# Differential attention: scores from two 64-row halves, keys and queries of a head kept on chip

## The chip, the cores and the metric

The kernel runs on one core of one Trainium2 chip. The metric is device time in microseconds (us) of one execution; the median of 3 runs is given, and one further execution is profiled.

## The reference, cut to what matters

The program is a two-layer backbone of a diffusion model: layer 0 mixes tokens by differential attention, layer 1 by a state-space scan, each followed by an MLP. Only the attention core of layer 0 is changed. There are 8 heads, 1024 latent tokens and 256 context tokens. Each head has two components `c` with 64 rows (`ATTN_HD`), whose softmaxes are subtracted:

```python
def attend(q, k, v):
    s = jnp.einsum('bqhcd,bkhcd->bhcqk', q, k).astype(jnp.float32)
    p = jax.nn.softmax(s, axis=-1)
    w = p[:, :, 0] - lam * p[:, :, 1]
    o = jnp.einsum('bhqk,bkhe->bqhe', w.astype(v.dtype), v)
    return rmsnorm(o, subln_g) * (1.0 - lambda_init)
```

Everything is in float32. The kernel gets this from TensorE by splitting each operand into a rounded high part and the remainder (`hi`, `lo`, type fp32r): a product of two operands is hi·hi + hi·lo + lo·hi, three matmuls (`mm3`, lines 131 to 134).

## The kernel before

The changed part is `phase_b`. It runs over 72 units in program order, 9 for each head: unit u=0 takes the 256 context queries against the 256 context keys, units u=1 to 8 take 128 latent queries each against all 1280 keys. The loop is inside `manual()`, so on TensorE, VectorE, ScalarE and GpSimd the instructions stand in the order in which the code writes them.

One unit, in the order of the code:

- `scores` (lines 575 and 581): both components. K of a component is a tile of 128 rows, the 64 hi rows above the 64 lo rows; Q comes in two forms, `r=0` (hi above lo) and `r=1` (lo above hi). Two 128-row matmuls for each piece of at most 512 keys then sum four products, lo·lo among them. A unit with u>0 has 12 matmuls, 8 of 512 columns and 4 of 256, component 0 first.
- `maxima` (590, 594): VectorE copies the scores of a component from PSUM and takes the row extreme; `exps` (601, 604): ScalarE's exponential of each component; `combine` (612 to 615): VectorE subtracts.
- In the *next* unit the combined weights are transposed by TensorE (622, 627) in three parts, T0 (four 128x128 transposes), T1 (two) and T2 (four), and taken out of PSUM by `w_evac`: T0 by ScalarE (hi, 635) and VectorE (lo, 636), T1 and T2 by a ScalarE copy (640) and two GpSimd operations (641, 642).
- `values`: the `mm3` of the transposed weights of two units with V, 30 matmuls of 256 columns (6 after u=0). It stands behind the scores in units u = 1, 4, 6 and 8 (the 6 in u=2). Units u = 3, 5, 7 and 0 have none.
- Projections of the next head's Q and K (`proj_group`, 24 matmuls) fill TensorE between the transposes in u = 0, 1, 2, 3, 5 and 7 (`AHEAD`, `FILLS`); in head 7 the first part of the output projection does.

The place of `w_evac` differs. In most units T0 is taken out right behind its transposes, ahead of the exponentials in ScalarE's queue. In units with 30-matmul `values` ("late" in the code) it stands behind both exponentials and behind `combine`.

PSUM is one tile `PS` of 4096 columns: 8 banks of 512. Component 0 of the scores takes columns 0 to 1279, component 1 columns 1280 to 2559 (banks 0 to 4). T0 and most T2 go to bank 5, `values` and T1 to bank 6, projections (and T2 where there is no projection) to bank 7.

K and Q go through DRAM: `proj_group` splits them into a staging tile `stg` and writes them to `Kd` and `Qd` (`out`), and `load_k` and `load_q` read them back in the stacked forms, K of component 1 of the next head and the first two Q tiles behind the scores of u=8.

Of the kernel before, what the change touches and what calls it, by code (L numbers as in the profile page):

```python
# [10 lines left out]
ALU = mybir.AluOpType  # L11
# [59 lines left out]
class Prog:  # L71
# [430 lines left out]

    def proj_group(self, h, T, g, wt):
# [7 lines left out]
        q, sw, qc, s = self.rq, self.rs, self.rc, self.stg[:, :, 0:n]  # L511

        def product(k):
            return lambda: self.mm3(b, wt[k][0], wt[k][1], hT[0][:, k], hT[1][:, k], k == 0, k == 7)

        def out():
            dst = self.Kd if T else self.Qd
            for c in range(2):
                self.dma(dst[h % 2, c, :, c0 : c0 + n].rearrange("(l r) n -> r l n", l=2),
                         s[64 * c : 64 * c + 64].bitcast(F32))  # L520

        def direct():
            nc.scalar.activation(s[:, 0], b, AF.Copy, scale=scale)
            nc.vector.scalar_tensor_tensor(s[:, 1], b, scale, s[:, 0].bitcast(F32), ALU.mult, ALU.subtract)
            out()

        def evac():
            nc.scalar.activation(q, b, AF.Copy, scale=scale)
            nc.vector.scalar_tensor_tensor(qc, b, scale, self.cosT[:, t], ALU.mult, ALU.mult)
            for j in range(4):  # L530
                self.dma(sw[32 * j : 32 * j + 32], q[32 * (j ^ 1) : 32 * (j ^ 1) + 32])

        def sine():
            nc.gpsimd.tensor_tensor(sw, sw, self.sinT[:, t], ALU.mult)

        def add():
            nc.vector.tensor_tensor(qc, qc, sw, ALU.add)

        def store():
            self.split(s[:, 0], s[:, 1], qc)  # L540
# [25 lines left out]


    def scores(self, u, Q, K):
        mm = self.nc.tensor.matmul
        if u == 0:  # L570
            for t in range(2):
                for c in range(2):
                    o = self.PS[:, 512 * t + 256 * c : 512 * t + 256 * c + 256]
                    for r in range(2):
                        mm(o, Q[:, c, r, 128 * t : 128 * t + 128], K[c][:, 0:256], start=r == 0, stop=r == 1)
            return
        qs = slice(128 * ((u - 1) % 2), 128 * ((u - 1) % 2) + 128)
        for c in range(2):
            for k0, k1 in (((0, 512), (512, 1024), (1024, 1280)), ((0, 256), (256, 768), (768, 1280)))[c]:
                for r in range(2):  # L580
                    mm(self.PS[:, 1280 * c + k0 : 1280 * c + k1], Q[:, c, r, qs], K[c][:, k0:k1], start=r == 0, stop=r == 1)  # L581


    def maxima(self, u, p, sm):
        ts = self.nc.vector.tensor_scalar
        if u == 0:
            for t in range(2):
                for c in range(2):
                    i = 512 * t + 256 * c
                    ts(p[c][:, 256 * t : 256 * t + 256], self.PS[:, i : i + 256], 1.0, None, ALU.mult, ALU.min,  # L590
                       accum_out=sm[:, 2 * t + c : 2 * t + c + 1])
        else:
            for c in range(2):
                ts(p[c], self.PS[:, 1280 * c : 1280 * c + 1280], 1.0, None, ALU.mult, ALU.min, accum_out=sm[:, c : c + 1])  # L594

# [21 lines left out]
    def w_part(self, u, w, n, tb):  # L617

        if u == 0:
            for kt in range(2):  # L620
                for t in range(2):
                    self.nc.tensor.transpose(tb[:, 256 * kt + 128 * t : 256 * kt + 128 * t + 128],
                                             w[:, 256 * t + 128 * kt : 256 * t + 128 * kt + 128], self.ident)
            return shaped(tb, (2, 256)), self.wT[0][:, 0:2], self.wT[1][:, 0:2]
        k0, k1 = ((0, 4), (4, 6), (6, 10))[n]
        for kt in range(k0, k1):
            self.nc.tensor.transpose(tb[:, 128 * (kt - k0) : 128 * (kt - k0) + 128],  # L627
                                     w[:, 128 * kt : 128 * kt + 128], self.ident)
        qs = slice(128 * ((u - 1) % 2), 128 * ((u - 1) % 2) + 128)
        return shaped(tb[:, 0 : 128 * (k1 - k0)], (k1 - k0, 128)), self.wT[0][:, k0:k1, qs], self.wT[1][:, k0:k1, qs]  # L630

    def w_evac(self, tb, hi, lo, direct):
# [4 lines left out]
        else:  # L637
            m, n = tb.shape[1:]
            t = shaped(self.wraw.next()[:, 0 : m * n], (m, n))
            nc.scalar.activation(t, tb, AF.Copy)  # L640
# [11 lines left out]
    def b_start(self):  # L652
# [4 lines left out]
        self.wr = Ring([(self.rv(4 * i, 4, 128), self.rv(4 * i + 2, 4, 128)) for i in range(3)])  # L657
        self.stg = self.rv(12, 2, 512)
        self.qb = Ring([self.bank(i) for i in (4, 5)])
# [4 lines left out]
        for split, T in zip(splits, (1, 0)):  # L664
            split(0)
            wt = split(1)
            for g in (2, 0, 1):
                products, rest = self.proj_group(0, T, g, wt)
                for f in products:
# [9 lines left out]
    def phase_b(self):  # L679
# [6 lines left out]
        self.raw = Ring([self.wv(0, 1024)])  # L686
        Kr = Ring([self.view(self.R1, 5 * i, (1280,)) for i in range(3)])
        Vr = Ring([self.rv(36 + 5 * i, 10, 128) for i in range(3)] + [self.view(self.R1, 15, (10, 128))])
        Qr = Ring([self.rv(51 + 4 * i, 2, 2, 256) for i in range(2)])
        self.wT = self.rv(16, 10, 256), self.rv(26, 10, 256)  # L690
        pb = self.bank(6)
        loaded = {}

        def load_k(h, c):
            K = loaded[h, "k", c] = self.rv(0, 1280) if (h, c) == (7, 1) else Kr.next()
            for k0, k1 in ((0, 256), (256, 1280)):
                self.dma(K[:, k0:k1].bitcast(F32), self.Kd[h % 2, c, :, k0:k1])
# [6 lines left out]
        def load_q(h, pair):  # L704
            Q = Qr.next()
            cols = slice(256 * pair, 256 * pair + 256)
            self.dma(Q[:, :, 0].bitcast(F32), self.Qd[h % 2, :, :, cols].rearrange("c r n -> r c n"))
            for hl in range(2):
                self.dma(Q[64 * hl : 64 * hl + 64, :, 1].bitcast(F32),
                         self.Qd[h % 2, :, 64 - 64 * hl : 128 - 64 * hl, cols].rearrange("c r n -> r c n"))  # L710
            loaded[h, pair] = Q

# [95 lines left out]
        wsums, wt6 = Ring([self.wv(0, 512), self.wv(2, 512)]), []  # L808
        wregs = [(self.view(t, x, (2, 512)), self.view(t, x + 4, (2, 512))) for t, x in ((self.R1, 0), (self.R, 8), (self.R, 36))]
        wraw6 = [shaped(self.wv(x, 1024), (2, 512)) for x in (0, 8, 12)]  # L810
# [41 lines left out]
        self.qb = Ring([self.bank(7)])  # L852
        load_k(0, 0)
        load_k(0, 1)
        load_q(0, 0)
        load_q(0, 1)
        load_v(0)
# [17 lines left out]
        with self.manual():  # L875
            for n in range(72 + 5):
# [10 lines left out]
                if front:  # L887
                    K = loaded[h, 'k', 0], loaded[h, 'k', 1]
                    pair = (u + 1) // 2
                    Q = loaded[h, pair]  # L890
# [1578 lines left out]
    def run(self):  # L2469
        tc = self.tc  # L2470
        pool = lambda name, **kw: tc.tile_pool(name=name, bufs=1, **kw)
        with pool("cst") as self.cst, pool("psp", space=bass.MemoryType.PSUM) as psp, \
             pool("drp", space=bass.MemoryType.DRAM) as drp, pool("hp") as hp:
            dt = lambda name, *shape: drp.tile(list(shape), F32, name=name)
            self.PS = psp.tile([128, 4096], F32, name="PS")
            self.Kd, self.Qd = dt("Kd", 2, 2, 128, 1280), dt("Qd", 2, 2, 128, 1280)
            self.Vd = dt("Vd", 8, 2, 128, 10, 128)
# [17 lines left out]
            with pool("r0") as rp, pool("fc") as cp:  # L2495
# [6 lines left out]
                with pool("r1") as rp, pool("f1") as fp:  # L2502
                    self.R1, self.F1 = rp.tile([128, 20 * KB], F32R, name="R1"), fp.tile([128, int(25.5 * KB)], F32, name="F1")
                    self.phase_b()
# [74 lines left out]
```

## Time and profile before

| | us |
|---|---|
| median of 3 runs (2848.01 to 2848.93) | 2848.92 |
| span of the profiled execution | 2849.8 |
| units of `phase_b`, first scores of head 0 to the end of head 7 | 222.7 to 852.4 |
| of it one head, by 8 | 78.7 |
| matmuls of `scores` in the program (lines 575, 581) | 64 + 768 |

How to read the rows of the profile: times are from the span's start. A row of the timeline has start, duration, engine, line and operation, written tile and read tiles, and a count where neighbours of one line were merged; idle time ahead of an instruction stands in brackets with what ended it. PE is TensorE's matmuls, PEld its weight loads, DVE VectorE, ACT ScalarE, POOL GpSimd. A matmul's duration holds its latency, so in a dense stream the distance from start to start tells the rate. PEclk is the granted share of TensorE's clock.

### The profile page before, as it was taken

The page shows a single profiled execution, that of the slowest core. Times are in us where ns is not written, and L with a number is a line of the kernel's source. Part 1 is how long each engine was busy: PE and PEld are TensorE (multiplying, and loading weights), DVE is VectorE, ACT ScalarE, POOL GpSimd, SP SyncE. Part 2 cuts the span into 40 slices and gives each one's busy share as a digit, 9 for nine tenths or more (in the row PEclk, how much of TensorE's full clock was granted, in tenths as well). Part 3 has the DMA queues.
Part 4 walks back from the last instruction along what each step waited for, and adds up shares of the span by engine and source line. Part 5 has one row for each costly group of instructions (what it writes and reads, how often), then busy time and mean ns, then how long its engine had stood idle before and what let it go on. Part 6 is the DMA issues. An engine that isn't in the chain of part 4 may idle for free.

```text
span 2849.8 us, 43385 instructions
## 1 busy us (share of the span) xinstructions
PE 2723.3 (96%) x15229; PEld 2283.1 (80%) x15229; DVE 2019.8 (71%) x2984; ACT 1369.5 (48%) x2583; POOL 1037.2 (36%) x901
## 2 busy tenths in 40 slices
PE   6999999999999999999999999789999999999999
PEld 4688888888877887778877878688887778888887
DVE  6357788888873667767698878799543597668466
ACT  3425555565653753333444445487444633344443
POOL 3314676766663600000030013688121143336414
PEclk9999999999999999999999999899999999999999
DMA  9955555655825359886799878579742144476544
GB/s 279 319 172 188 152 173 172 177 171 171 256 91 182 128 179 316 294 302 216 249 312 310 272 238 263 169 228 306 235 154 98 66 163 160 155 246 227 167 131 142
DMA packets 414823, 586.30 MB, mean 206 GB/s; under 512 B 41870, under 2 KB 260236, under 8 KB 411404
## 3 DMA queue, kind: packets, MB, share of 16 engines
q1 hardware_dynamic: 414604, 583.52, 63.5%
q8 instruction: 120, 1.97, 0.3%
q14 instruction: 99, 0.81, 0.1%
HBM read 396.38 MB, written 182.82 MB: 203 GB/s over the span
## 4 chain that ended last, share of the span: by engine, by line
PE 76%; DVE 9%; DMA 5%; issue 4%; POOL 3%; ACT 2%; SPq 1%; DVEq 0%; ACTq 0%; POOLq 0%
PE PS L132 21%; PE PS L134 20%; PE PS L133 20%; PE PS L581 4%; PE PS L627 2%; PE PS L1928 2%; PE PS L1963 2%; DMA FU<-in_mlp_w 1%; DMA Ta<-FU 1%; PE PS L202 1%; DVE R L138 1%; SPq L80 1%; DVE F L615 1%; ACT F L604 1%; DVE H L138 1%
## 5 line engine op out<-in xcount | busy, mean ns | idle before, releaser
L132 PE MATMUL PS<-H 128*128 128x512 f32 x1072 | 420.6, 393 | 2.7 <-ACT H L137 1.7
L134 PE MATMUL PS<-H 128*128 128x512 f32 x1072 | 417.5, 390 | 2.8 <-DVE H L138 1.5
L133 PE MATMUL PS<-H 128*128 128x512 f32 x1072 | 417.7, 390 | 0.0
L132 PE MATMUL PS<-H,R 128*128 128x512 f32 (+1 forms) x828 | 308.0, 374 | 4.3 <-ACT R L137 2.0
L133 PE MATMUL PS<-H,R 128*128 128x512 f32 (+1 forms) x828 | 298.6, 361 | 0.0
L134 PE MATMUL PS<-H,R 128*128 128x512 f32 (+1 forms) x828 | 298.0, 361 | 0.0
L132 PEld LDWEIGHTS PS<-H 128*128 128x128 f32 x1072 | 201.2, 188 | 50.5 <-issue 6.4
L134 PEld LDWEIGHTS PS<-H 128*128 128x128 f32 x1072 | 201.2, 188 | 46.1 <-DVE H L138 2.3
L133 PEld LDWEIGHTS PS<-H 128*128 128x128 f32 x1072 | 201.3, 188 | 40.6
L604 ACT ACTIVATE F<-F,stat 128x1280 f32<-128x1280 f32 x128 | 174.3, 1362 | 106.6 <-DVE F L594 106.5
L137 ACT ACTIVATE H<-U 128x640 fp32r<-128x640 f32 x216 | 131.9, 674 | 172.6 <-PE PS L133 138.3
L137 ACT ACTIVATE R<-W 128x512 fp32r<-128x512 f32 (+1 forms) x184 | 128.7, 707 | 174.1 <-PE PS L133 101.5
L132 PE MATMUL PS<-R,H 128*128 128x512 f32 x520 | 208.0, 401 | 3.3 <-ACT H L137 3.3
L134 PE MATMUL PS<-R,H 128*128 128x512 f32 x520 | 205.0, 396 | 1.8 <-DVE H L138 1.8
L133 PE MATMUL PS<-R,H 128*128 128x512 f32 x520 | 204.5, 394 | 0.0
L138 DVE TENSOR_TENSOR H<-U,H 128x640 fp32r<-128x640 f32 x216 | 165.1, 797 | 50.6 <-ACT H L137 49.6
L138 DVE TENSOR_TENSOR H<-W,H 128x512 fp32r<-128x512 f32 (+1 forms) x137 | 125.2, 924 | 102.8 <-ACT H L137 102.1
L594 DVE TENSOR_SCALAR_CACHE_REDUCE F<-PS 128x1280 f32<-128x1280 f32 x128 | 185.2, 1483 | 9.3 <-PE PS L581 9.1
L137 ACT ACTIVATE H<-W 128x512 fp32r<-128x512 f32 (+2 forms) x158 | 95.4, 613 | 188.7 <-PE PS L133 116.8
L132 PEld LDWEIGHTS PS<-H,R 128*128 128x128 f32 x828 | 157.6, 191 | 30.2 <-issue 4.1
L134 PEld LDWEIGHTS PS<-H,R 128*128 128x128 f32 x828 | 157.0, 190 | 25.2 <-issue 0.8
L641 POOL TENSOR_SCALAR R<-F 128x256 fp32r<-128x256 f32 (+1 forms) x128 | 126.5, 989 | 136.0 <-ACT F L640 122.4
(534 smaller groups left out, 6860.0 us busy)
## 6 DMA issues: line engine op xcount, KB each, us to landing
W<-in_mlp_w SPq DMA_DIRECT2D x176, 256.0 KB
U<-Aa SPq DMA_DIRECT2D x108, 320.0 KB
Aa<-FU SPq DMA_DIRECT2D x91, 320.0 KB
Ad<-F SPq DMA_DIRECT2D x112, 256.0 KB
W<-Ad SPq DMA_DIRECT2D x112, 256.0 KB
FU<-in_mlp_w SPq DMA_DIRECT2D x32, 512.0 KB
Ta<-FU SPq DMA_DIRECT2D x16, 1024.0 KB
U<-in_ada_w SPq DMA_DIRECT2D x32, 512.0 KB
```

What stands on the lines that cost most here:

```text
L132: mm(out, ah, bh, start=first, stop=False, **kw)
L133: mm(out, ah, bl, start=False, stop=False, **kw)
L134: mm(out, al, bh, start=False, stop=last, **kw)
L137: self.nc.scalar.activation(hi, src, AF.Copy)
L138: (lo_eng or self.nc.vector).tensor_tensor(lo, src, hi.bitcast(F32), ALU.subtract)
L581: mm(self.PS[:, 1280 * c + k0 : 1280 * c + k1], Q[:, c, r, qs], K[c][:, k0:k1], start=r == 0, stop=r == 1)
L594: ts(p[c], self.PS[:, 1280 * c : 1280 * c + 1280], 1.0, None, ALU.mult, ALU.min, accum_out=sm[:, c : c + 1])
L604: nc.scalar.activation(p[c], p[c], AF.Exp, bias=sm[:, c : c + 1], scale=-1.0, accum_out=sn[:, 0:1] if c else s0[:, u + 1 : u + 2])
L627: self.nc.tensor.transpose(tb[:, 128 * (kt - k0) : 128 * (kt - k0) + 128], w[:, 128 * kt : 128 * kt + 128], self.ident)
L641: nc.gpsimd.tensor_scalar(hi, t, 1.0, 0.0, ALU.mult, ALU.add)
L1928: mm(b[:, o : o + 160], X[:, d, i, 64 * j : 64 * j + 128], U[:, 4 * n + i, cols], start=True, stop=True)
L1963: mm(o, cs[d][n % 2][j][:, i], W[:, d, i], start=False, stop=d == 1 and j == 1)
```

## The change

K and Q of a head no longer go through DRAM (but for head 0): `proj_group` writes hi and lo straight to resident tiles, `Ks[h % 2]` (two heads) and `Qs` (one), in which rows 0 to 63 are component 0 and rows 64 to 127 component 1. The staging tile, `load_k` and `load_q` go, and with them 228 DMAs of the program.

`scores` takes each component from its own 64 rows: hi·hi, hi·lo and lo·hi, three 64-row matmuls for each piece in the place of two 128-row ones, 18 for a unit with u>0 (12 for u=0; 8 before). `score_order` alternates the components, so that neighbouring matmuls mostly use different halves of TensorE's rows and different PSUM banks. For that component 1 moves from column 1280 to column 1536: component 0 has banks 0 to 2, component 1 banks 3 to 5. Bank 5 is no longer free; T0 and T2 now go to `spare`, the last 256 columns of bank 2 and of bank 5. Tiles in SBUF are laid out anew.

```diff
     def proj_group(self, h, T, g, wt, stage=None):
...
+        if stage is None:
+            hi, lo = (x[:, c0 : c0 + n] for x in (self.Ks[h % 2] if T else self.Qs))
+        else:
+            hi, lo = stage[:, 0, 0:n], stage[:, 1, 0:n]
...
         def out():
-            dst = self.Kd if T else self.Qd
-            for c in range(2):
-                self.dma(dst[h % 2, c, :, c0 : c0 + n].rearrange("(l r) n -> r l n", l=2),
-                         s[64 * c : 64 * c + 64].bitcast(F32))
+            if stage is not None:
+                for l, t_ in enumerate((hi, lo)):
+                    self.dma((self.Kd if T else self.Qd)[l, :, c0 : c0 + n], t_.bitcast(F32))
...
+    def score_order(self):
+        items = []
+        for c, chunks in ((0, ((1024, 1280), (0, 512), (512, 1024))), (1, ((0, 512), (512, 1024), (1024, 1280)))):
+            at = c / 8
+            for k in chunks:
+                for j in range(3):
+                    items.append((at, c, k, j))
+                    at += (k[1] - k[0]) / 512
+        return [x[1:] for x in sorted(items)]
...
     def scores(self, u, Q, K):
         mm = self.nc.tensor.matmul
+        half = lambda t, c, k: t[64 * c : 64 * c + 64, k]
+        pairs = ((0, 0), (0, 1), (1, 0))
...
-        qs = slice(128 * ((u - 1) % 2), 128 * ((u - 1) % 2) + 128)
-        for c in range(2):
-            for k0, k1 in (((0, 512), (512, 1024), (1024, 1280)), ((0, 256), (256, 768), (768, 1280)))[c]:
-                for r in range(2):
-                    mm(self.PS[:, 1280 * c + k0 : 1280 * c + k1], Q[:, c, r, qs], K[c][:, k0:k1], start=r == 0, stop=r == 1)
+        qs = slice(128 + 128 * u, 256 + 128 * u)
+        for c, (k0, k1), j in self.order:
+            a, b = pairs[j]
+            mm(self.PS[:, 1536 * c + k0 : 1536 * c + k1], half(Q[a], c, qs), half(K[b], c, slice(k0, k1)), start=j == 0, stop=j == 2)
...
             for c in range(2):
-                ts(p[c], self.PS[:, 1280 * c : 1280 * c + 1280], 1.0, None, ALU.mult, ALU.min, accum_out=sm[:, c : c + 1])
+                ts(p[c], self.PS[:, 1536 * c : 1536 * c + 1280], 1.0, None, ALU.mult, ALU.min, accum_out=sm[:, c : c + 1])
...
         for kt in range(k0, k1):
-            self.nc.tensor.transpose(tb[:, 128 * (kt - k0) : 128 * (kt - k0) + 128],
+            i = kt - k0
+            self.nc.tensor.transpose(tb[:, i // 2, 128 * (i % 2) : 128 * (i % 2) + 128],
...
+        r1 = lambda off, *dims: self.view(self.R1, off, dims)
+        self.Ks = [(r1(10 * i, 1280), r1(10 * i + 5, 1280)) for i in range(2)]
+        self.Qs = self.rv(49, 1280), self.rv(54, 1280)
+        self.order = self.score_order()
+        self.spare = shaped(self.PS[:, 0:3072], (2, 1536))[:, :, 1280:1536]
...
-                        load_k(h + 1, 0)
-                    if u % 2 == 0 and u < 8 and (h, pair + 1) not in loaded:
-                        load_q(h, pair + 1)
...
-                    self.scores(u, Q, K)
-                    if u == 8 and h < 7:
-                        load_k(h + 1, 1)
-                        load_q(h + 1, 0)
-                        load_q(h + 1, 1)
+                    self.scores(u, self.Qs, self.Ks[h % 2])
...
-                        tb = pb[:, 256:512] if part == 1 else self.bank(7 if part == 2 and not groups else 5)
+                        tb = (shaped(pb[:, 256:512], (1, 256)) if part == 1 else
+                              shaped(self.bank(7), (2, 256)) if part == 2 and not groups else self.spare)
```

Three places in the built programs, with the semaphores that each instruction waits for. TensorE in unit 3 of head 3, a unit without `values`, before: the scores (581), T0 (627), the first products of the projection.

```order
L581 MATMUL PS<-R_1850,R_110 128x512 [waits DMAHW7_49]
L581 MATMUL PS<-R_1850,R_110 128x512 [waits DMAHW1_49,DMAHW0_49]
L581 MATMUL PS<-R_1850,R_110 128x512 x2
L581 MATMUL PS<-R_1850,R_110 128x256 x4
L581 MATMUL PS<-R_1850,R_110 128x512 x4
L627 MATMUL PS<-ident,F_1851 128x128 [waits DVE_49,Activation_49]
L627 MATMUL PS<-ident,F_1851 128x128 x3
```

The same place after: 596 are the scores, 643 is T0.

```order
L596 MATMUL PS<-R_1850,R_110 128x256 [waits Activation_49]
L596 MATMUL PS<-R_1850,R_110 128x512
L596 MATMUL PS<-R_1850,R_110 128x256 x2
L596 MATMUL PS<-R_1850,R_110 128x512 x10
L596 MATMUL PS<-R_1850,R_110 128x256
L596 MATMUL PS<-R_1850,R_110 128x512
L596 MATMUL PS<-R_1850,R_110 128x256 x2
L643 MATMUL PS<-ident,F_1851 128x128 [waits DVE_49]
L643 MATMUL PS<-ident,F_1851 128x128
L643 MATMUL PS<-ident,F_1851 128x128 [waits DVE_49]
L643 MATMUL PS<-ident,F_1851 128x128
```

The DMA waits are gone. The first score matmul waits for ScalarE: by its count for the copy of the previous unit's T2 out of `spare`. T0 is now two pairs, one for each bank of `spare`, and each waits for VectorE: by the counts, the first pair for the maxima of component 0 of this same unit (which read bank 2), the second for those of component 1 (bank 5). Before, the count was that of the `combine` of the unit before.

ScalarE in unit 5 of head 3, before: T0's hi (635), exponential of component 0 (604), T1's copy (640), exponential of component 1, T2's copy.

```order
L635 ACTIVATE R_110<-PS 128x4x128 [waits DVE_49,PE_49]
L604 ACTIVATE F_1851,FC<-F_1851,stat 128x1280 [waits DVE_49]
L640 ACTIVATE F_1851<-PS 128x256 [waits PE_49,Pool_49]
L604 ACTIVATE F_1851,stat<-F_1851,stat 128x1280 [waits DVE_49]
L640 ACTIVATE F_1851<-PS 128x512 [waits DVE_49,PE_49,Pool_49]
```

After (653 is T0's hi, 619 an exponential, 658 a copy):

```order
L653 ACTIVATE R_110<-PS 128x4x128 [waits DVE_49,PE_49]
L619 ACTIVATE F_1851,FC<-F_1851,stat 128x1280
L658 ACTIVATE F_1851<-PS 128x256 [waits PE_49,Activation_49,Pool_49]
L619 ACTIVATE F_1851,stat<-F_1851,stat 128x1280
L658 ACTIVATE F_1851<-PS 128x512 [waits DVE_49,PE_49,Pool_49]
```

The order is the same, but the exponentials have no wait of their own any more: the T0 copy ahead of them waits for the maxima of both components already.

TensorE at the border of units 4 and 5 of head 3, before: ten transposes of T0, T1 and T2 at the end of a "late" unit, then the next scores.

```order
L627 MATMUL PS<-ident,F_1851 128x128 [waits DVE_49]
L627 MATMUL PS<-ident,F_1851 128x128 x5
L627 MATMUL PS<-ident,F_1851 128x128 [waits DVE_49]
L627 MATMUL PS<-ident,F_1851 128x128 x3
L581 MATMUL PS<-R_1850,R_110 128x512 [waits DMAHW4_49,DVE_49]
```

After:

```order
L643 MATMUL PS<-ident,F_1851 128x128 [waits DVE_49]
L643 MATMUL PS<-ident,F_1851 128x128
L643 MATMUL PS<-ident,F_1851 128x128 [waits DVE_49]
L643 MATMUL PS<-ident,F_1851 128x128 x7
L596 MATMUL PS<-R_1850,R_110 128x256 [waits DVE_49]
```

By the counts, the VectorE wait of the first scores was for the maxima of the unit before; now it is for T0's lo (654), which in a late unit stands in VectorE's queue behind `combine`. Outside `phase_b` and the last rows ahead of it the engines' orders are the same.

More of the change, by code (lines that the diff above doesn't have):

```diff
@@ L539, in store @@
         def store():
-            self.split(s[:, 0], s[:, 1], qc)
+            self.split(hi, lo, qc)
             out()
@@ L686, in phase_b @@
         self.raw = Ring([self.wv(0, 1024)])
[L687 to L690, printed above, removed]
+        r1 = lambda off, *dims: self.view(self.R1, off, dims)
+        self.Ks = [(r1(10 * i, 1280), r1(10 * i + 5, 1280)) for i in range(2)]
+        self.Qs = self.rv(49, 1280), self.rv(54, 1280)
+        Vr = Ring([self.rv(32 + 5 * i, 10, 128) for i in range(3)] + [r1(20, 10, 128)])
+        self.wT = self.rv(12, 10, 256), self.rv(22, 10, 256)
+        self.order = self.score_order()
+        self.spare = shaped(self.PS[:, 0:3072], (2, 1536))[:, :, 1280:1536]
         pb = self.bank(6)
         loaded = {}
[L694 to L697, printed above, removed]
         def load_v(h):
@@ L702, in load_v @@
                 self.dma(V[j].bitcast(F32), self.Vd[h, j])
[L704 to L711, printed above, removed]
         def values(h, pair):
@@ L852, in phase_b @@
         self.qb = Ring([self.bank(7)])
[L853 to L856, printed above, removed]
+        for k0, k1 in ((0, 256), (256, 1280)):
+            for dst, src in ((self.Qs, self.Qd), (self.Ks[0], self.Kd)):
+                for l in range(2):
+                    self.dma(dst[l][:, k0:k1].bitcast(F32), src[l, :, k0:k1])
         load_v(0)
```

44 lines of the change are left out of this document (22 added, 22 removed).

## The prediction

> **What bounds the kernel now.** I read the page's busy time first, then busy time by stretch with one stretch per head, then the waits of TensorE inside the attention phase (222 to 853 us), and last the timeline of single units. In the second row the columns after the length are busy us (and instructions) of PE, PEld, DVE, ACT and POOL, then the granted clock.
>
> ```profile
> PE 2723.3 (96%) x15229; PEld 2283.1 (80%) x15229; DVE 2019.8 (71%) x2984; ACT 1369.5 (48%) x2583; POOL 1037.2 (36%) x901
> ...
> 528.59:606.93 78.34, 74.77 (x483) 66.56 (x481) 65.64 (x101) 46.78 (x96) 53.32 (x51) 1.00 0.59 170
> ...
> PE PS L627 <- DVE R L636: 12.3, 14, 1.5
> ...
> PE PS L575 <- DMA R<-Kd: 10.0, 6, 2.2
> ```
>
> TensorE bounds the phase: in head 4 it is busy for 74.8 of 78.3 us. In the whole phase it waits 12 us for T0's lo copy and 10 us for K from DRAM. VectorE (65.6) is not far behind. So a shorter score block would come straight off the time, and so would any new wait of TensorE be added to it.
>
> One unit without `values` (head 3, u=3) shows how the engines lean on each other:
>
> ```profile
> 480.55 2.49 PE L581 MATMUL PS<-R,R 128*128 128x512 f32 x12
> ...
> 482.32 1.48 DVE L594 TENSOR_SCALAR_CACHE_REDUCE F<-PS 128x1280 f32<-128x1280 f32 x1
> ...
> 482.88 0.60 PE L627 MATMUL PS<-ident,F 128*128 128x128 f32 x4
> ...
> 483.51 0.60 ACT L635 ACTIVATE R<-PS 128x512 fp32r<-128x512 f32 x1 [1.65 <-PE PS L627]
> ...
> 483.73 1.49 DVE L594 TENSOR_SCALAR_CACHE_REDUCE F<-PS 128x1280 f32<-128x1280 f32 x1
> ...
> 484.01 1.36 ACT L604 ACTIVATE F<-F,stat 128x1280 f32<-128x1280 f32 x1
> ...
> 485.36 0.37 ACT L640 ACTIVATE F<-PS 128x256 f32<-128x256 f32 x1
> ...
> 485.62 1.36 ACT L604 ACTIVATE F<-F,stat 128x1280 f32<-128x1280 f32 x1
> ...
> 487.09 0.60 ACT L640 ACTIVATE F<-PS 128x512 f32<-128x512 f32 x1
> ...
> 487.21 2.57 PE L581 MATMUL PS<-R,R 128*128 128x512 f32 x12
> ```
>
> T0 (627) starts 2.33 us after the first score matmul, in the middle of the first maxima: nothing ties it to this unit's scores. The second maxima ends only at 485.22, 4.67 after the start.
>
> **The score block.** Rows of u=6 of head 3 (first scores at 505.18, see below), a burst of weight loads, and the group of matmuls that use 32 columns of the array:
>
> ```profile
> 506.86 1.49 DVE L594 TENSOR_SCALAR_CACHE_REDUCE F<-PS 128x1280 f32<-128x1280 f32 x1 [0.18 <-PE PS L581]
> ...
> 507.59 0.28 PE L132 MATMUL PS<-R 128*128 128x256 f32 x1
> ...
> 511.07 1.01 PEld L627 LDWEIGHTS PS<-ident,F 128*128 128x128 f32 x9
> ...
> L273 PE MATMUL PS<-U,scT 128*32 128x128 f32 x512 | 15.6, 274 | 0.3 <-DVE modc L282 0.3
> ```
>
> The block takes 507.59 - 505.18 = 2.41 us for 5120 columns, near 0.23 us per 512. The new one has 18 matmuls with 7680 columns. Upper end, if the halves run one after another: 12 x 0.23 + 6 x 0.12 = 3.5 us. Lower end, if they run side by side and hide their weight loads: half the columns, 7.5 x 0.23 = 1.7. No 64-row pair is in this trace. The nearest row is L273: 512 matmuls of 274 ns in 15.6 us, 30 ns each, so parts of the array do run side by side. The weight loads are then the limit: nine in 1.01 us, (1.01 - 0.19) / 8 = 0.10 each, 18 of them 1.9 us. I take 1.9, a gain of 0.5 us a unit where the block is on the path, with 1.7 and 3.5 as ends.
>
> The Trainium skill, "TensorE: Matmul & The Clock Gate", section on LDWEIGHTS, speaks against the halves: a load costs by its columns, not its rows, so 64 rows save nothing; by its figure 18 loads would be an estimated 1.9 us. No run here shows a 64-row load. Its page "TensorEngine Tiling (Array Packing)", section Tiling Modes, says that a change of tiling mode drains the engine. This trace cannot show it for rows; a drain would be at most a matmul's latency, 0.39 - 0.23 = 0.16 us, twice a unit, 23 us in 72 units, and none of it where PE stands idle next to the block anyway.
>
> The maxima of component 0 start at 1.68 now, some 0.45 after the middle of the block. In the new order the last matmul of component 0 is the 16th of 18: 15 x 0.105 + 0.39 + 0.25 = 2.2. I call this start m = 2.2 (3.6 if the halves run one after another).
>
> **The new waits.** In the new program T0 lies in banks 2 and 5, and its two pairs wait for the two maxima of the same unit. That a bank, not a column, decides is to be seen in the trace of before (head 7, u=2):
>
> ```profile
> 779.54 1.48 DVE L594 TENSOR_SCALAR_CACHE_REDUCE F<-PS 128x1280 f32<-128x1280 f32 x1
> ...
> 781.08 0.50 PE L581 MATMUL PS<-R,R 128*128 128x256 f32 x2 [0.21 <-DVE F L594]
> ```
>
> The 256-column matmuls (columns 1024 to 1279) waited for the maxima of columns 1280 to 2559: only bank 2 is common.
>
> Type A, units without long `values` (u = 2, 3, 5, 7). The second pair of T0 can start at m + 1.41 (start to start of the two maxima) + 1.49 + 0.06 = m + 2.96 = 5.2 us. Behind it on TensorE wait T1, T2, all projections and the next scores. ScalarE holds its T0 copy, which now waits too, ahead of both exponentials.
> - u=3: T0's second pair 5.2 to 5.6, copy 0.60, then as in the rows exponential 1.35, T1 copy 0.26, exponential 1.47, so the last ends at 9.3; T2's copy 0.60, at 9.9, which the next scores wait for (bank 2). Before: 487.21 - 480.55 = 6.66. **+3.2**.
> - The others are full of projections; from T0 to the unit's end stays, less 0.22 for the first pair.
>
> ```profile
> 461.22 2.47 PE L581 MATMUL PS<-R,R 128*128 128x512 f32 x12
> ...
> 470.42 2.49 PE L581 MATMUL PS<-R,R 128*128 128x512 f32 x12
> ...
> 473.47 0.60 PE L627 MATMUL PS<-ident,F 128*128 128x128 f32 x4
> ...
> 505.18 2.57 PE L581 MATMUL PS<-R,R 128*128 128x512 f32 x12
> ...
> 512.18 2.58 PE L581 MATMUL PS<-R,R 128*128 128x512 f32 x12
> ...
> 514.60 0.60 PE L627 MATMUL PS<-ident,F 128*128 128x128 f32 x4
> ...
> 521.68 2.47 PE L581 MATMUL PS<-R,R 128*128 128x512 f32 x12
> ...
> 528.59 0.48 PE L575 MATMUL PS<-R,R 128*128 128x256 f32 x2
> ...
> 531.24 0.97 PE L575 MATMUL PS<-R,R 128*128 128x256 f32 x6 [2.17 <-DMA R<-Kd]
> ...
> 532.41 0.66 PE L627 MATMUL PS<-ident,F 128*128 128x128 f32 x4 [0.19 <-DVE R L636]
> ```
>
> u=2: T0 at 473.47, end 480.55, 7.08; new 5.2 + 6.86 = 12.1 for 10.13, **+1.9**. u=7 likewise 12.1 for 9.50, **+2.6**. u=5 (T0 at 498.00, next row, end 505.18): 5.2 + 6.96 = 12.2 for 10.95, **+1.2**.
>
> Type B, late units (u = 1, 4, 6, 8). `values` covers T0's wait here (1.9 + 3.6 = 5.5 us against 5.2), but the *next* scores need bank 2, and so T0's lo, which stands behind `combine`. Units 4 and 5 of head 3:
>
> ```profile
> 490.92 1.48 DVE L594 TENSOR_SCALAR_CACHE_REDUCE F<-PS 128x1280 f32<-128x1280 f32 x1
> ...
> 494.23 2.57 PE L581 MATMUL PS<-R,R 128*128 128x512 f32 x12
> ...
> 495.79 1.55 DVE L615 SCALAR_TENSOR_TENSOR F<-F,stat 128x1280 f32<-128x1280 f32 x1
> ...
> 497.26 0.68 DVE L636 TENSOR_TENSOR R<-PS,R 128x512 fp32r<-128x512 f32 x1
> ...
> 498.00 0.66 PE L627 MATMUL PS<-ident,F 128*128 128x128 f32 x4 [1.20 <-DVE R L636]
> ```
>
> From the first maxima to TensorE's release by the lo copy it is 498.00 - 490.92 = 7.1 us. Before, only T0 of u=5 met this wait, 3.8 us into the unit; now the scores do. A late unit so lasts m + 7.1 = 9.3: u=6 for 7.00 and u=8 for 6.91, **+2.3 and +2.4**. In u=4 VectorE still has the `combine` of u=3: its maxima started 3.8 us after u=3's last exponential (490.92 - 487.09), new 9.3 + 3.8 - 9.9 = 3.2, so 10.3 for 7.02, **+3.3**. u=1, held up the same way, 10.3 for 9.20, **+1.1**.
>
> u=0 gains: no wait for K (2.17), T0's first pair at 2.4 behind the third small maxima in the place of 3.82, **-1.4**.
>
> Sum for a head: -1.4 + 1.1 + 1.9 + 3.2 + 3.3 + 1.2 + 2.3 + 2.6 + 2.4 = +16.6; eight heads +133 us. Head 0 has no K wait to lose and head 7 other fills; I leave both in the mean. The other edits I cost at nothing: the 228 DMAs fewer lie beside TensorE's work (only the K wait was seen by it), the T0 copies read as many elements, and the resident Q columns are rewritten after their last reader.
>
> **The clock.** Stalls of this length have a price of their own. Stretches of 3.41 us with PE's busy time, count and granted clock:
>
> ```profile
> 448.73:452.14 3.41, 1.74 (x13) 1.00 0.70 212
> 452.14:455.55 3.41, 2.72 (x9) 0.50 0.99 321
> 575.02:578.43 3.41, 2.21 (x12) 1.00 0.12 41
> 578.43:581.84 3.41, 3.41 (x21) 1.00 0.73 179
> ```
>
> A stretch with 1.74 us busy is followed by one at half clock, one with 2.21 is not. In the new units TensorE stands still for about 3 us between scores and T0 (u = 3, 5, 7) and for 2.7 to 3.2 at the end of u = 4, 6 and 8, with 1.9 us of work between. A half-clock stretch costs 1.7 us of full work. Ends: none, and nine a head, 8 x 9 x 1.7 = 122 us. I take a little under four a head on the path, 50 us.
>
> **Total.** The profiled span is 2849.8; 2849.8 + 133 + 50 = 3033. The median is 0.9 below the span, so 3032.
>
> **Rivals.**
> - The clock stays up (18%): the score block and the stalls alone, 2982. For it: head 4 kept 1.00 through its 2.17 us for K, and 1.74 busy is the one edge shown. Against: the new stalls are longer and come in pairs.
> - The halves run one after another (14%): m rises by 1.4 in about seven units of nine, 8 x 7 x 1.4 = +78, with somewhat fewer slow stretches: 3095. For it: no row shows row halves.
> - The waits bind only in part (8%), say because the maxima come earlier than I place them: half the stalls, about 2910.
> - Faster (5%): T0's wait is over when TensorE gets there, in all units, as it is in the late ones by 0.3 us. It decides in u = 2, 3, 5 and 7: the second maxima would have to end before 1.9 us (2.7 in u=2) and the lo copy before the next scores. Then 64 blocks give 0.5 each and K's wait 10: 2849 - 32 - 10 = 2807. Against it: a maxima alone takes 1.48.
> - The change does not do what it says: the program has the 64-row matmuls at rows 0 and 64; only their overlap is open, see above.
>
> **Chances.** The forecast, near 3032, has 55%. The range reaches from between the partly binding waits and the steady clock to past the serial halves: 2950 to 3105. Faster by over 0.2% (what a measurement can tell from no change) 5%; within it 2%, out of the partly binding case; slower 93%.
>
> **What would show it.** In the profile after: T0 (643) idle before it, ended by the maxima (609), about 3 us in u = 3, 5 and 7; the scores (596) idle 2 to 3 us for the lo copy (654) and, after u=3, for the ScalarE copy (658); heads of 95 to 102 us; PE's busy share in the phase near 75%; a granted clock visibly below 1.00; no wait on Kd. A score block of 1.9 us would show the loads as the limit, 3.5 serial halves. I am wrong if T0 starts before the second maxima ends, or if scores start before the lo copy.

## The result and the profile after

| | before | after |
|---|---|---|
| median, us | 2848.93 (2848.01 to 2850.22, 4 runs) | 3036.06 (3034.1 to 3038.67, 4 runs) |
| ratio | | 1.0653, 95% interval 1.0638 to 1.0669 |
| span of the profiled execution | 2849.8 | 3032.2 |
| first scores of head 0 to first scores of head 7 | 540.8 | 707.3 |

The change costs 187 us. The predicted 3032 is 4 us off. The page of the changed kernel, busy time, granted clock in 40 slices, and the groups of the maxima (609) and of the transposes (643):

```profile
PE 2788.7 (92%) x15645; PEld 2326.4 (77%) x15645; DVE 2008.7 (66%) x2984; ACT 1369.7 (45%) x2583; POOL 1015.5 (33%) x901
...
PEclk9998889988898999999999999989999999999999
...
L609 DVE TENSOR_SCALAR_CACHE_REDUCE F<-PS 128x1280 f32<-128x1280 f32 x128 | 185.6, 1487 | 69.1 <-PE PS L596 69.1
...
L643 PE MATMUL PS<-ident,F 128*128 128x128 f32 x640 | 114.2, 298 | 83.0 <-DVE F L609 74.1
```

The eights of the clock lie in slices 4 to 13 (75.8 us each), within the attention phase, and T0's transposes wait 74 us for the maxima, which they did not before. The waits of TensorE within the phase (222 to 1040 us; total, number, longest), and head 4 in the busy time by stretch, whose last columns are granted clock, DMA share and GB/s:

```profile
PE PS L643 <- DVE F L609: 74.1, 64, 1.7
PE PS L596 <- DVE R L654: 40.6, 20, 3.9
PE PS L591 <- DVE R L654: 16.0, 7, 2.4
PE PS L643 <- DVE F L605: 7.3, 7, 1.1
PE PS L591 <- DMA Qd<-R: 5.8, 1, 5.8
PE PS L637 <- DVE F L609: 5.2, 4, 1.7
```

```profile
624.41:727.09 102.68, 84.44 (x532) 73.13 (x532) 63.55 (x102) 46.86 (x96) 50.65 (x51) 0.88 0.22 66
```

The waits for K are gone; waits for maxima and for T0's lo copy (654) stand in their place. The head takes 102.7 us for 78.3, and its clock is 0.88 for 1.00. The timeline of TensorE in head 2, unit 3, and in units 6 and 7, where the clock was full:

```profile
460.40 2.02 PE L596 MATMUL PS<-R,R 64*128 64x256 f32 x18
463.98 0.44 PE L643 MATMUL PS<-ident,F 128*128 128x128 f32 x2 [1.56 <-DVE F L609]
465.39 0.44 PE L643 MATMUL PS<-ident,F 128*128 128x128 f32 x2 [0.97 <-DVE F L609]
...
470.08 0.50 PE L596 MATMUL PS<-R,R 64*128 64x256 f32 x3 [0.40 <-ACT FC L739]
...
495.61 2.00 PE L596 MATMUL PS<-R,R 64*128 64x256 f32 x18
501.23 1.25 PE L643 MATMUL PS<-ident,F 128*128 128x128 f32 x10
504.72 2.01 PE L596 MATMUL PS<-R,R 64*128 64x256 f32 x18 [2.24 <-DVE R L654]
508.33 0.44 PE L643 MATMUL PS<-ident,F 128*128 128x128 f32 x2 [1.59 <-DVE F L609]
509.74 0.44 PE L643 MATMUL PS<-ident,F 128*128 128x128 f32 x2 [0.97 <-DVE F L609]
...
516.75 0.50 PE L596 MATMUL PS<-R,R 64*128 64x256 f32 x3
```

T0's two pairs wait 1.6 and 1.0 us, each for its own maxima; the scores of unit 7 wait 2.2 us for the lo copy of unit 6.

### The profile page after: what moved, and what is told of

Its sections match the earlier page's. It is cut to its first block, busy times and chain, and to the rows that moved or that the text cites. A ratio compares the mean times of both kernels' runs of the same rounds, so it can differ in the third digit from the quotient of the medians.

```text
span 3032.2 us, 43765 instructions
## 1 busy us (share of the span) xinstructions
PE 2788.7 (92%) x15645; PEld 2326.4 (77%) x15645; DVE 2008.7 (66%) x2984; ACT 1369.7 (45%) x2583; POOL 1015.5 (33%) x901
## 3 DMA queue, kind: packets, MB, share of 16 engines
q8 instruction: 123, 2.02, 0.3%
## 5 line engine op out<-in xcount | busy, mean ns | idle before, releaser
L132 PE MATMUL PS<-H,R 128*128 128x512 f32 (+1 forms) x828 | 329.3, 400 | 5.6 <-ACT R L137 2.2
L133 PE MATMUL PS<-H,R 128*128 128x512 f32 (+1 forms) x828 | 317.6, 384 | 0.0
L134 PE MATMUL PS<-H,R 128*128 128x512 f32 (+1 forms) x828 | 315.3, 381 | 0.0
L659 POOL TENSOR_SCALAR R<-F 128x256 fp32r<-128x256 f32 (+1 forms) x128 | 115.4, 902 | 333.0 <-ACT F L658 296.3
L132 PEld LDWEIGHTS PS<-H,R 128*128 128x128 f32 x828 | 170.5, 206 | 34.2 <-issue 4.3
L138 DVE TENSOR_TENSOR H<-W,H 128x512 fp32r<-128x512 f32 (+1 forms) x137 | 126.0, 930 | 103.4 <-ACT H L137 102.9
L134 PEld LDWEIGHTS PS<-H,R 128*128 128x128 f32 x828 | 170.2, 206 | 28.9 <-issue 0.8
L643 PE MATMUL PS<-ident,F 128*128 128x128 f32 x640 | 114.2, 298 | 83.0 <-DVE F L609 74.1
```

Source lines behind the costliest of these rows:

```text
L132: mm(out, ah, bh, start=first, stop=False, **kw)
L133: mm(out, ah, bl, start=False, stop=False, **kw)
L134: mm(out, al, bh, start=False, stop=last, **kw)
L138: (lo_eng or self.nc.vector).tensor_tensor(lo, src, hi.bitcast(F32), ALU.subtract)
L643: self.nc.tensor.transpose(tb[:, i // 2, 128 * (i % 2) : 128 * (i % 2) + 128], w[:, 128 * kt : 128 * kt + 128], self.ident)
L659: nc.gpsimd.tensor_scalar(hi, t, 1.0, 0.0, ALU.mult, ALU.add)
```

## The experiments

Two theories were to be told apart: the new waits by bank cost the time, with the slow clock that they bring (the prediction), or the 64-row matmuls do. All medians stand against 2849 to 2854 of the kernel before on the same chip; intervals are of the ratio to it. Rows of different chips carry this difference, up to 6 us, between them. The last columns are worked out from the traces for heads 0 to 6: mean length of a head and of units 0, 5 and 6 (from first score matmul to first score matmul), sum of TensorE's gaps of more than 0.15 us, and number of 3.41-us stretches at clock 0.50, each worth up to 3.41 x 0.5 = 1.7 us.

| kernel | median, us | interval | head | u=0 | u=5 | u=6 | gaps | slow stretches |
|---|---|---|---|---|---|---|---|---|
| before | 2848.9 | | 77.3 | 10.7 | 10.7 | 7.0 | 21 | 2 |
| after | 3036.1 | 1.064 to 1.067 | 101.0 | 13.0 | 14.4 | 9.1 | 127 | 45 |
| own_bank | 2878.4 | 1.008 to 1.011 | 80.1 | 11.9 | 12.4 | 6.8 | 30 | 11 |
| only_banks | 2951.0 | 1.034 to 1.037 | 90.5 | 11.5 | 15.5 | 7.0 | 68 | 22 |
| sequence | 3012.2 | 1.055 to 1.059 | 98.3 | 12.0 | 15.3 | 9.1 | 81 | 28 |
| fill_first | 2964.8 | 1.039 to 1.043 | 92.1 | 14.2 | 10.4 | 9.1 | 100 | 21 |
| bank2_last | 3022.6 | 1.058 to 1.063 | 99.6 | 13.1 | 17.3 | 6.8 | 116 | 39 |
| lo_first | 3027.8 | 1.059 to 1.063 | 99.3 | 13.1 | 16.1 | 7.7 | 124 | 41 |
| free_bank6 | 2930.9 | 1.026 to 1.029 | 86.0 | 11.5 | 10.4 | 9.1 | 66 | 17 |
| all_three | 2905.6 | 1.017 to 1.021 | 83.5 | 12.3 | 12.3 | 6.8 | 52 | 8 |
| warm | 3012.4 | 1.053 to 1.058 | 98.2 | 13.3 | 14.5 | 9.1 | 67 | 26 |
| own_sequence | 2895.0 | 1.012 to 1.017 | 81.9 | 10.1 | 10.6 | 7.8 | 13 | 2 |
| best | 2884.8 | 1.008 to 1.013 | 80.3 | 10.8 | 9.3 | 7.7 | 46 | 3 |
| mixed | 2877.3 | 1.008 to 1.011 | 79.3 | 10.7 | 12.7 | 6.8 | 33 | 2 |

### The halves without the bank waits, and the bank waits without the halves

`own_bank`, from the changed kernel:

```diff
-    (1, ((0, 512), (512, 1024), (1024, 1280)))
+    (1, ((256, 768), (768, 1280), (0, 256)))        # PS column 1280 * c + k0
...
+            if (c, k0, j) == (0, 1024, 2):
+                self.nc.scalar.activation(self.fence, self.PS[:, 1024:1025], AF.Copy)
...
-        self.spare = shaped(self.PS[:, 0:3072], (2, 1536))[:, :, 1280:1536]
+        self.spare = shaped(self.bank(5), (2, 256))
```

> The changed kernel, but component 1 of the scores is back at column 1280 and T0 and T2 are back in bank 5, which nothing else uses; the row halves still alternate. Both halves now write bank 2 (component 0 first, component 1 in the last three matmuls), and a one-column ScalarE copy between them orders the two. Theory of the bank waits: T0 is no longer tied to this unit's maxima nor the next scores to T0's lo copy, so both waits of TensorE go, and with them the half-speed stretches; what is left is the shorter score block and no K wait: about 2810 us (2790 to 2850), heads near 76 us, granted clock in the phase near 1.00. Rival, the 64-row matmuls themselves (drains between row halves, 18 loads for 12) cost the time: still over 2950.

`only_banks`, from the kernel before: component 1 at column 1536 in pieces from 0, 512 and 1024; T0 and T2 in `spare`.

> The kernel before, with only its places in PSUM changed to those of the changed kernel: component 1 at column 1536, T0 and T2 in the last 256 columns of banks 2 and 5. Scores stay 128-row matmuls, K and Q still go through DRAM. Theory of the bank waits: nearly the whole loss appears. The maxima start at 1.68 for 2.03 us, so each wait is some 0.35 us shorter than in the changed kernel (72 units, about -20 us), the block is 0.6 longer where it is on the path, the waits for K stay: about 3020 us (2980 to 3060), with TensorE idle before T0 for the second maxima and before the scores for T0's lo copy. Rival, the 64-row matmuls cost the time: no more than 2870.

Without the bank waits 158 of the 187 us go, with the same 64-row matmuls in alternation: the first theory holds. The gain over the kernel before that was expected (2810) did not come. The 29 left stand mostly in two units, u=0 (+1.2) and u=5 (+1.6); the others lie within 0.3 of before. Much of both is slow clock. In u=0 every head has a slow stretch, two of seven had one before; u=5 takes 13.0 us in the five heads with one there, and 11.5 in head 6 without, against 10.9 before. In u=5 the one-column copy is late, since ScalarE still has the last unit's exponential and copies:

```profile
504.99 1.76 PE L596 MATMUL PS<-R,R 64*128 64x256 f32 x14
508.57 0.74 PE L596 MATMUL PS<-R,R 64*128 64x256 f32 x4 [1.82 <-ACT lamc L598]
```

The bank waits alone cost 102 us, not the 171 expected. The late units kept 7.0 us: four matmuls of component 0, in banks 0 and 1, run ahead of the wait for the lo copy (unit 7 of head 3, below), while the alternating order writes bank 2 at once. So the other 85 us come with the new scores: in the late units, where the waits meet the new order of the pieces, and through 23 more slow stretches. That is argued, no run isolates it.

```profile
562.89 1.17 PE L581 MATMUL PS<-R,R 128*128 128x512 f32 x4
564.42 1.67 PE L581 MATMUL PS<-R,R 128*128 128x256 f32 x8 [0.36 <-DVE R L639]
```

### The order of the components, and work in the gaps

`sequence` and `own_sequence` sort the 18 matmuls by component, in the changed kernel and in `own_bank`:

```diff
-        return [x[1:] for x in sorted(items)]
+        return [x[1:] for x in sorted(items, key=lambda x: (x[1], x[0]))]
```

> The changed kernel with the same 18 matmuls, all of component 0 first, then all of component 1. If the alternation makes the row halves run side by side, the last score matmul of a unit starts near 3.2 us in the place of 1.73, the second maxima starts near 3.9 in the place of 3.45, T0's second pair near 5.45 in the place of 5.0, and each unit gets about 0.45 us longer: 64 x 0.45 = 29 and some clock, about 3070 us. If the halves do not overlap, or the order does not matter, the block stays near 1.8 us and the time within 10 us of 3036.

> The kernel with a bank of its own for T0 (bank 5, one-column copy between the halves), with the components in sequence and not in alternation. Without the bank waits TensorE is busy in all units but u=0, so the 0.92 us by which the sequence makes the block longer should now be seen in the time: u = 1 to 8 each longer by 0.9, less what u=5 idles anyway: 8 x 7 x 0.9 = 50 us more than 2878, about 2928 us (2900 to 2950). Rival, the length of the block lies beside other engines' work as it did with the bank waits: 2878 or less.

The halves do run side by side: in sequence the block lasts 587.82 - 584.96 = 2.86 us (unit 6 of head 3, below), in alternation 1.94. They overlap in part even in sequence, since 2.86 is less than the 3.5 that the prediction gave for one half after the other. But the sequence made the changed kernel 24 us faster. Component 0 is first and is done no later, the first maxima starts at 586.98 - 584.96 = 2.02 as in the changed kernel, and the second follows it, not its scores. The longer block only fills what was idle, and 28 stretches are slow for 45.

```profile
584.96 2.93 PE L596 MATMUL PS<-R,R 64*128 64x256 f32 x18
586.98 1.49 DVE L609 TENSOR_SCALAR_CACHE_REDUCE F<-PS 128x1280 f32<-128x1280 f32 x1 [0.70 <-PE PS L596]
587.82 0.39 PE L132 MATMUL PS<-R 128*128 128x256 f32 x1
```

With a bank for T0 the alternation is worth 17 us (11, when each kernel is taken against the kernel before on its own chip), not 50: in sequence five units get 0.9 longer and two 0.5, but u=0 and u=5 give 1.8 each back, with 2 slow stretches for 11.

`fill_first` runs `fills[0]` ahead of T0 in u = 2, 3, 5 and 7; `warm` puts 22 matmuls there whose result nothing reads:

```diff
+                warm = (lambda n: [mm(pb[:, 258:384], self.Ks[h % 2][0][:, 0:128], self.Ks[h % 2][0][:, 0:126], start=True, stop=True)
+                                   for i_ in range(n)]) if front and u in (2, 3, 5, 7) else (lambda n: None)
+                warm(12)
...
+                        t = self.w_part(prev[1], prev[2], part, tb, lambda: warm(10) if part == 0 else None)
```

> The changed kernel, with the first projection products of u = 2, 3, 5 and 7 (9 matmuls, 12 in u=3) moved ahead of T0, into the time in which TensorE waits for the maxima. Theory of the bank waits: T0's second pair stays at 5.0 us, but about 2.1 us of work is done before it: u=2, 5 and 7 get 2.1 us shorter, u=3 stays (its end is set by ScalarE's copy of T2): 7 heads x 3 x 2.1 = 44 us, and two or three half-speed stretches a head go with the idle time, another 25 to 40: about 2960 us (2930 to 2995). Rival, the 64-row matmuls cost the time: within 10 us of 3036.

> The changed kernel, with 22 matmuls of 126 columns added in u = 2, 3, 5 and 7 (12 ahead of T0's first pair, 10 between its pairs), whose result nothing reads: they fill the time in which TensorE waits for the maxima and do nothing else. The waits are as long as before, so all that goes is the slow clock behind them. In the changed kernel 45 stretches at half speed fall into heads 0 to 6, and cost about 75 us there; some 25 of them follow these four units. Theory (the slow clock is a price of its own): 25 x 1.7 = 42 us go, about 2990 us (2970 to 3015). Rival (the slow stretches lie in slack and cost nothing): within 10 us of 3036, or longer by the added matmuls where T0 is not waiting.

Work in the gaps gave 71 us, as expected. `warm` gave 24 where 42 were expected: 19 slow stretches went, but in u=2 the added matmuls moved T0 back by 0.4 us. So the slow clock is a price of its own, of at least 24 us; the 45 stretches bound it by 45 x 1.7 = 77 in these heads. The price of one can be read in the changed kernel: u=3 takes 9.7 us in the two heads at full clock and 11.1 to 11.2 in the five with one slow stretch, 1.5 more, though its T0 starts at the same place.

### The wait of the late units

```diff
# bank2_last
-        for c, chunks in ((0, ((1024, 1280), (0, 512), (512, 1024))), ...
+        for c, chunks in ((0, ((0, 512), (512, 1024), (1024, 1280))), ...
# lo_first
+                    if late and part == 1:
+                        evac()
                     if front and part == 1:
...
                         self.combine(u, p, s0, sn)
-                    if late and part == 1:
-                        evac()
```

> The changed kernel, with the score pieces of component 0 in the order of component 1: columns 0 to 511, 512 to 1023, 1024 to 1279, so that bank 2 is written last and not first. Theory: after a late unit (u = 1, 4, 6, 8) TensorE then has twelve score matmuls, some 1.4 us, to do before it meets the wait for T0's lo copy. 1.4 us times four units times eight heads is 43 us, and a part of the half-speed stretches on top: about 2985 us (2960 to 3005). Rival, the wait for the lo copy is not what holds the late units (the maxima or the exponentials behind it are): within 10 us of 3036.

> The changed kernel, with one edit in the late units: T0's lo copy stands ahead of combine in VectorE's queue and not behind it. Theory: the next scores are released some 1.5 us earlier, and the combine that moves back by 0.7 us is still in time for T0 of the next unit: 1.5 x 4 x 8 = 48 us and a part of the half-speed stretches: about 2975 us (2945 to 3000). Rival, as before: the lo copy is not what holds these units: within 10 us of 3036, or slower by the later combine (0.7 x 32 = 22 us).

Both missed: 13 and 8 us, not 50 to 60, although u=6 got shorter by 2.3 and 1.4. A unit is counted from its first score matmul, so a wait that comes behind this matmul counts for the next unit: in `bank2_last` u=5 got 2.9 longer. Nor did that edit do what it was meant to:

```profile
596.05 0.50 PE L596 MATMUL PS<-R,R 64*128 64x512 f32 x1
598.36 3.10 PE L596 MATMUL PS<-R,R 64*128 64x512 f32 x17 [1.82 <-DVE R L654]
```

One matmul runs ahead of the wait, not twelve. The second one writes columns 1536 to 2047, bank 3, where T0 has nothing: as this wait reads, the program orders T0's view by its whole stretch of columns, 1280 to 3071. No run tests that further. In `lo_first` the wait moved on. The waits of TensorE in its phase:

```profile
PE PS L643 <- DVE F L609: 93.4, 65, 3.9
PE PS L643 <- DVE F L605: 22.1, 7, 3.2
PE PS L596 <- DVE R L654: 16.0, 15, 2.1
...
PE PS L637 <- DVE F L609: 5.9, 4, 2.4
PE PS L591 <- DVE R L654: 3.4, 7, 0.5
```

For the lo copy they fell from 56.6 to 19.4 us, for the maxima they rose from 86.6 to 121.4: `combine` is now behind the lo copy, and the maxima behind `combine`.

### Other banks for T0

`free_bank6` puts T0 of units without long values in bank 6; `all_three` joins it with the two edits above; `best` frees the late units too, and moves in u=2 only the copy out of bank 6; `mixed` mends `own_bank`:

```diff
# free_bank6
+                        tb = (shaped(pb, (2, 256)) if part == 0 and not late else
+                              shaped(pb[:, 256:512] if late else self.PS[:, 1280:1536], (1, 256)) if part == 1 else
...
# best: as free_bank6, and in u = 4, 6, 8
+                              shaped(self.bank(7), (2, 256)) if swap and part == 0 ...
...
+                        if late and not groups:
+                            ready.insert(0, ready.pop())
# mixed, from own_bank: T0 of u = 0, 5, 7 in bank 6, T1 in bank 5; in u=5
...
+                        for f in fills[0]:
+                            f()
+                        self.scores(u, self.Qs, self.Ks[h % 2], True)    # the last three
+                        self.maxima(u, p, sm)
```

> The changed kernel with T0 of the units without long values (u = 0, 2, 3, 5, 7) in bank 6, which values leave free there, and T1 of these units in the free columns of bank 2; in u=2 the short values are taken out of bank 6 before T0 instead of at the end of the unit. Theory: the wait of T0 for the maxima goes in these units (u=2 and u=7 shorter by about 2, u=3 by 3, u=5 by 3, u=0 by 1.5 to 2: 12 us a head, 96 in all, most of the half-speed stretches within), the waits of the late units stay: about 2925 us (2895 to 2955). Rival, the row halves cost the time: over 3000.

> The last three edits together. Theory: both kinds of bank wait are gone, the alternating halves stay. Units as in the run with a bank of its own for T0, without its ScalarE copy between the halves: heads near 77 us, about 2835 us (2805 to 2860), granted clock in the phase near 1.00. Rival, the change between 64-row and 128-row matmuls and the fuller VectorE keep it from gaining: 2850 to 2890.

> An attempt at a layout without either wait. T0 of u = 0, 2, 3, 5, 7 lies in bank 6 and T1 in the free columns of bank 2, as in the earlier run, but in u=2 only the copy out of bank 6 is moved, so that nothing of the computation changes. In u = 4, 6 and 8 T0 lies in bank 7 (no projection there), T2 in the free columns of banks 2 and 5, and ScalarE copies T2 first. The next scores then wait for T2's copy, some 0.3 us, and no longer for T0's lo copy (2.3): from 2931 some 45 us of waits and 10 to 20 of slow clock go: about 2870 us (2845 to 2900). If the alternating halves are worth more than the changes between 64 and 128 rows cost, it can come under the kernel before (2849); I give that one chance in four.

> The kernel with a bank of its own for T0, with the two units mended in which it is slower than the kernel before (u=0 11.9 for 10.7 us, u=5 12.4 for 10.7). In u = 0, 5 and 7 T0 goes to bank 6 and T1 to bank 5, so that T0 does not wait for the lo copy of the last T0; in u=5 the three score matmuls that wait for the one-column copy stand behind T0 and the first projection products. Theory (these two units hold all that is lost against the kernel before, the alternating block itself gains 0.1 to 0.2 us a unit): u=5 near 9.9, u=0 near 11.2, the others as they were, 76.8 us a head for 80.1: 2878 - 26 = 2852 us (2835 to 2870), level with the kernel before. Rival, the loss is spread over the units by the changes between 64 and 128 rows: 2870 to 2880.

In `free_bank6` and `all_three` the edit in u=2 also overwrites the squares of one pair of each head before they are summed, so that pair is normed by another's squares and their result is wrong; the instructions are as many and as large. `free_bank6` lands where expected (2931): T0's wait alone, with the slow clock behind it, was worth 105 us. The other three come out 15 to 70 us above what was expected, and above the kernel before. In `best` the scores still wait for T2's copy (14.2 us in 14 waits) and for T0's lo copy (11.3 in 7), and u=1 takes 10.1 us for 8.7. In `mixed` u=0 is mended, but u=5 is not: TensorE stands still for the one-column copy, and again since T2 shares a bank with T1, whose copy is late; head 7, which the table leaves out, is 9 us longer than in `own_bank`.

```profile
506.87 0.63 PE L647 MATMUL PS<-ident,F 128*128 128x128 f32 x4 [1.61 <-ACT lamc L600]
...
513.93 0.66 PE L647 MATMUL PS<-ident,F 128*128 128x128 f32 x4 [1.35 <-ACT F L662]
```

No version beat the kernel before. What is left open is whether a layout exists in which the alternation pays; in `own_bank` it brought at most 0.2 us a unit, in five of the nine.

## Why the prediction was right, point by point

**The waits by bank (right).** T0's second pair started 4.99 us into unit 3 (460.40 to 465.39; predicted 5.2), that unit lasted 9.68 (9.9), unit 7 12.03 (12.1), unit 6 9.11 (9.3): m is 2.02, not 2.2. Unit 5 took 12.1 (12.2) where its clock was full, in two heads of `warm`. `own_bank` takes 158 of 187 us away with these waits and what follows from them.

**The clock (right mechanism, too small).** 50 us were taken, a little under four slow stretches a head; there were 45 in seven heads, 6.4 a head, against 2 before. What made up for it is that the waits were sized 0.1 to 0.7 us a unit too long (u=1: 9.6 for 10.3). So it is partly luck that the total is only 4 us off. An estimate from heads 0 to 6, which lost 707.3 - 540.8 = 166.5 us: 43 more slow stretches at 1.5 are 64, where 44 were taken, and the waits are the other 102, where 7 x 16.6 = 116 were.

**The score block (right size by luck, wrong limit, wrong gain).** The timeline of unit 6 of head 3, in `own_bank` and (T0 alone) before:

```profile
518.00 2.01 PE L596 MATMUL PS<-R,R 64*128 64x256 f32 x18
519.94 0.38 PE L132 MATMUL PS<-R 128*128 128x256 f32 x1
...
523.64 1.25 PE L645 MATMUL PS<-ident,F 128*128 128x128 f32 x10
524.82 1.54 PE L596 MATMUL PS<-R,R 64*128 64x256 f32 x12
```

```profile
511.17 1.25 PE L627 MATMUL PS<-ident,F 128*128 128x128 f32 x10
```

The block lasts 1.94 us (predicted 1.9), 0.47 less than the 2.41 before. But `values` takes 3.70 for 3.58, and from T0 to the next scores it is 1.18 for 1.01: 0.29 go at the two borders between 64-row and 128-row matmuls, and 0.18 stay (6.82 for 7.00). The prediction put these borders at nothing. The Trainium skill, "TensorEngine Tiling (Array Packing)", section Tiling Modes, says that a change of mode drains the engine; the trace agrees, with 0.29 us for the two changes of a unit. Weight loads were named as the limit, at 0.10 us each. They are not: the start of unit 0 in `own_bank`, whose matmuls are in the rows further below, has 12 64-row loads in 0.77 us, worked out as there (0.77 - 0.19) / 11 = 0.05 each.

```profile
541.84 0.77 PEld L591 LDWEIGHTS PS<-R,R 64*128 64x128 f32 x12 [0.17 <-issue]
```

What sets the block is then the columns of one half: its 9 matmuls have 3840, at 0.23 us per 512 these are 1.73, and some 0.2 go where the block begins and ends. That the wrong limit gave 1.9 as well is luck.

**u=0 and u=8 (right together), and the wait for K (worth nothing).** -1.4 us was taken for u=0 and +2.4 for u=8. Unit by unit both look wrong: u=0 got 2.3 longer, and u=8 did not change (6.8 for 6.9). But two matmuls of u=0, into banks 0 and 1, run ahead of the wait for the lo copy, so the wait that was placed at the end of u=8 counts for u=0. TensorE at the start of head 3, whose u=8 before it began at 516.75:

```profile
523.57 0.39 PE L591 MATMUL PS<-R,R 64*128 64x256 f32 x2
526.29 0.86 PE L591 MATMUL PS<-R,R 64*128 64x256 f32 x10 [2.33 <-DVE R L654]
528.24 1.12 PE L643 MATMUL PS<-ident,F 128*128 128x128 f32 x4 [1.09 <-DVE F L605]
```

The lo copy lets the scores go 526.29 - 516.75 = 9.5 us into u=8 (predicted 9.3), and T0 follows 1.95 later (2.4). With one slow stretch the two units take 20.3 us where 18.6 were predicted at full clock.

The wait for K by itself was worth nothing: even `own_bank`, without it, does not gain in u=0. Before, and in `own_bank`, the start of unit 0 and its T0:

```profile
449.01 0.48 PE L575 MATMUL PS<-R,R 128*128 128x256 f32 x2
451.10 0.98 PE L575 MATMUL PS<-R,R 128*128 128x256 f32 x6 [1.62 <-DMA R<-Kd]
452.83 1.11 PE L627 MATMUL PS<-ident,F 128*128 128x128 f32 x4 [0.75 <-DVE R L636]
```

```profile
541.84 0.97 PE L591 MATMUL PS<-R,R 64*128 64x256 f32 x12
545.65 0.66 PE L645 MATMUL PS<-ident,F 128*128 128x128 f32 x4 [2.84 <-DVE R L656]
```

T0 starts 3.82 us into the unit in the one and 3.81 in the other. The wait for K stood ahead of a longer one, for the lo copy behind `combine`; without it that one is longer, 2.84 in one piece for 0.75, and a slow stretch follows. The 10 us of K waits, which the rival "Faster" and the expectation of `own_bank` counted as a gain, were not on the path here. That step reads a wait's length as its worth.

**The rivals.** The serial halves were priced at +78 us by a later m; `sequence` shows m unmoved and the time 24 us lower, with halves that overlap in part. The steady clock (2982) fell with the 45 slow stretches.

**What would show it.** The waits, their lines and the heads of 95 to 102 us came as said (96.6 to 102.9); TensorE's busy share in head 4 is 84.4 of 102.7, 82% and not 75%; that work at half clock counts as busy for longer fits this, but no run isolates it.

## What to carry to other kernels

Before a matmul is made cheaper by a new PSUM layout, list which reader each bank then shares with which writer: here 0.2 us a unit was won and up to 3 us of bank waits were bought. A wait is worth what stands behind it, not its length, so price its removal at the next wait of the same chain. Idle time of TensorE costs twice when it slows the clock; work moved into the gap can then be worth more than a shorter block.

## What the runs showed of the hardware

A stretch need not be wholly idle for the clock to fall behind it. All fourteen traces were cut between 230 and 1000 us (the heads, and in the shorter traces some of what follows) into the 3.41-us stretches of the clock's rows. Of some 2340 full-speed stretches with up to 1.1 us of TensorE idle none was followed by a slow one, of some 305 with 1.1 to 2.1 us 104 were, and all of 136 with more. The Trainium skill, "TensorE: Matmul & The Clock Gate", section "Part 1: The HAM clock gate", names a whole idle window of about 3.4 us; here 2.1 us of it were always enough.
